# First mixer: low weight parts summed by DMA, and attention outputs weighed by pairs of heads

## The chip, the cores and the metric

The kernel runs on one core of one Trainium2 chip. The metric is the device time of one execution in microseconds (us); a lower time is better. TensorE (PE) does the matrix products, VectorE (DVE), ScalarE (ACT) and GpSimd (POOL) the elementwise work, and SyncE (SP) issues nearly all transfers.

## The reference

A small model of two blocks over 512 tokens of width 1024, all in float32. The first block has two layers; the change is in the first layer's mixer ("even mixer"), cut here to what matters:

```
z = rmsnorm(x) @ w_in                        # 1024 -> 512 (q) + 128 (k) + 128 (v) + 512 (u)
q, k = rope(q), rope(k)                      # 8 query heads, 2 key/value heads, width 64
s = q k^T / 8, only keys with |i - j| <= 128, softmax with one extra sink logit per head
p = exp(s - m) / (sum exp(s - m) + exp(sink - m))
ya = p @ v                                   # 8 heads x 64 = 512 columns
d  = centred mean of u over 2, 4, 8, 16 positions, minus u   # four groups of 128 columns
yb = (d @ w_pool[group]) * pool_scale        # 512 columns
x  = x + concat(ya, yb) @ w_out              # 1024 -> 1024
x  = x + relu(rmsnorm(x) @ w1)^2 @ w2        # 1024 -> 4096 -> 1024
```

A second layer with another mixer, a second block and a final norm follow; the change doesn't touch their code.

## The kernel before

**Products in three parts.** Each float32 factor is split into a high part (rounded to the fp32r type that TensorE takes) and a low part (the rest). A product is the sum of three matmuls, high x high, high x low and low x high (`mm3`, L561 records each), each with 128 weights columns and 512 tokens; in the trace they are `mm<-hi,wh`, `mm<-hi,wl` and `mm<-lo,wh`. Three such matmuls are called a triple here.

**Weight units.** Weights come from memory in units of 128 x 1024 (512 KB; 8 triples). `Unit.load` issues the transfer on SP's queue into one of 4 raw buffers (`wr`). `Unit.split` makes the two parts: a copy with rounding into `wh` (ACT or POOL, whichever the planner reckons sooner done) and then a subtract, raw minus high, into `wl` (DVE or POOL). `Weights.at` hands a unit's columns to the matmuls once `self.ready` covers them.

**Order of work.** Every engine runs its instructions in the order in which this program emits them. A planner (`_Flow`) decides on that order: it has a clock of its own, `fl.now`, which each matmul moves on, and costs for every elementwise instruction. Chains of elementwise work (generators) go on when their due time has come; `yield 0.1` means to look again 0.1 us of the planner's time later.

In the first mixer (phase "a") the main work is attention (`attend` over the eight `job0`), with up to 3 heads in flight. The dense products are the filling, in the list `fill = [q_blocks(), pooling(), out_proj("eout", yhl, 0)]`. `_Flow.run` takes a step of the filling whenever the main work makes no progress; `_Flow.step` tries only `fill[:self.wide]`, and `wide` is 1 in phase "a". Where that first generator can't go on either, the planner lets 0.1 us pass.

**When a unit is split.** The units stand in the list `order` in the order ein2, ein0, ein1, wpool, ein3, ein4, eout0 to eout3. `pump` drops a unit from the head of the list when it has been used up, and starts the split of those among the first three that it can:

```
while order and order[0].task is not None and order[0].left == 0:
    order.pop(0)
...
for i, u in enumerate(order[:AHEAD]):          # AHEAD = 3
```

`Weights.at` starts the split of a unit that is asked for and not yet begun. `wpool` (one unit of 512 columns) holds the matrices of the four pooling groups, one product for each, so it is used up only with the fourth. `pooling` runs over ein3 and ein4, a unit of 8 triples for each group; `pool_chain` then does that group's window sums, the difference, its split into parts, the product with `wpool` (put at the head of `fill`) and the split of the result into `yhl[g]`. The first half of `out_proj` needs all four `yhl[0..3]`, the second half the attention's `yhl[4..7]`.

**A head.** `Head.score` issues the score matmuls (`sc`), `expo` the row maximum (`mx`, `nm`, DVE) and the exponential with its row sum (`p<-sc,nm`, ACT). `finish` then adds the sink's part to the denominator, takes the reciprocal (`w4`) and calls `weigh`, four copies with a scale (`p<-p,w`, ACT or POOL) over blocks of 256 or 384 columns. `apply` waits for that (`self.done`); it transposes the probabilities (`tr<-cst,p`), splits them into parts (`ph` on ACT, `pl` on DVE) and multiplies with the values (`av`). `combine` and `store` gather two heads into one `ya` of 128 x 512 and split it into `yhl[4 + pair]`.

Of the kernel before, what the change touches and what calls it, by code (L numbers as in the profile page):

```python
# [13 lines left out]
AF = mybir.ActivationFunctionType  # L14
ALU = mybir.AluOpType
# [3 lines left out]
P = 128  # L19
# [3 lines left out]
NQ = T // P  # L23
# [33 lines left out]
_WT = {}  # L57
# [431 lines left out]
def tile_hybrid(ctx: ExitStack, tc: tile.TileContext, wt, xT, pT, prm_d, cst_d, out):  # L489
    nc = tc.nc  # L490
# [3 lines left out]
    fl = _Flow()  # L494
    go = fl.go
    V, S, G = (_Engine(fl, e, k) for e, k in ((nc.vector, "V"), (nc.scalar, "S"), (nc.gpsimd, "G")))
# [13 lines left out]
    def uid(s):  # L510
        cnt[0] += 1
        return f"{s}{cnt[0]}"

    def blk(name="b", dt=F32, n=T):
        return bp.tile([P, TB], dt, tag="b", bufs=NB, name=uid(name))[:, 0:n]

    def small(n, name="s", dt=F32):
        return sp.tile([P, n], dt, tag=f"s{n}", bufs=24, name=uid(name))
# [6 lines left out]
    def bank(tag):  # L525
        spare = len(banks) - sum(1 for k in held if k != tag and not held[k])
        if held[tag] >= getattr(fl, tag) or spare < 1 or min(banks) > fl.now:
            return None
        banks.remove(min(banks))
        held[tag] += 1  # L530
        return pp.tile([P, T], F32, tag="ps", bufs=8, name=uid(tag))
# [6 lines left out]
    def takec(tag):  # L538
        while (t := bank(tag)) is None:
            yield 0.1  # L540
        return t

    def give(tag):
        banks.append(max(fl.now, fl.last) + 0.1)
        held[tag] -= 1
# [6 lines left out]
    def waitc(*tasks):  # L552
        for t in tasks:
            while not t.done:
                yield 0.1

    def f(ap):
        return ap.bitcast(F32)
# [5 lines left out]
    def tr(o, i, idn):  # L564
        PE.transpose(o, i, idn)  # L565
        fl.now += 0.11
# [4 lines left out]
    def first(*engines):  # L571

        return min(engines, key=lambda e: max(e[0].free, fl.now) + e[1])[0]

    def width(ap):
        n = 1
        for d in ap.shape[1:]:
            n *= d
        return n

    def copy(out, src, scale=None):

        n, ps = width(out), src.space == PSUM
        sc = 1.0 if scale is None else scale
        e = first((S, 0.06 + n / 1090.0), *(() if ps else ((G, 0.07 + n * 0.00117 + fl.gc),)))
        if e is S:
            S.activation(out, src, AF.Copy, scale=sc)
        else:
            G.tensor_scalar(out, src, sc, 1.0, op0=ALU.mult, op1=ALU.mult)

    def tt(op, out, a, b, bias=None):

        n = width(out)
        if PSUM in (a.space, b.space):
            e = V
        else:
            e = first((V, 0.07 + n / 960.0), (G, 0.07 + n * 0.00227 + (fl.gt if bias is None else bias)))
        e.tensor_tensor(out, a, b, op=op)


    NRAW, NSPLIT, AHEAD = 4, 4, 3
    units, order = {}, []

    class Unit:
        def __init__(self, name, i, cuts=1):
            self.name, self.i = name, i
            t = _WT[name]
            self.n = min(1024, _WN[t][1] - 1024 * i)
            self.left = self.n
            self.raw = self.hi = self.lo = self.task = None  # L610
            self.parts = [(self.n * c // cuts, self.n * (c + 1) // cuts) for c in range(cuts)]
            self.at, self.ready = [], 0
            self.kept = None
# [48 lines left out]
        def split(self):  # L662
            while len(self.at) < len(self.parts):
                self.load()
            r = self.raw
            self.hi = wp.tile([P, 1024], F32R, tag="whi", bufs=NSPLIT, name=uid("wh"))
            self.lo = wp.tile([P, 1024], F32R, tag="wlo", bufs=NSPLIT, name=uid("wl"))
            wl["split"] += 1
            wl["due"] -= 1
            for (c0, c1), t in zip(self.parts, self.at):  # L670
                while fl.now < t:
                    yield 0.1
                copy(self.hi[:, c0:c1], r[:, c0:c1])
                yield
                tt(ALU.subtract, self.lo[:, c0:c1], r[:, c0:c1], f(self.hi[:, c0:c1]), fl.gw)
                if c1 == self.n:
                    wl["raw"] -= 1
                yield
                self.ready = c1

        def use(self, n):
# [4 lines left out]
    wl = {"raw": 0, "split": 0, "dma": 0.8, "due": 0}  # L686
# [89 lines left out]
    def C(name, n=None):  # L776
        o = _CO[name][0]
        n = n or _CO[name][1]
        if o + n <= NKEEP:
            return cst[:, o:o + n]  # L780
        t = blk("cst")
        nc.sync.dma_start(t[:, :n], cst_d[:, o:o + n])
        return t

    def PR(name, i=0, n=1):
        o, w = _PO[name]
        return prm[:, o + i:o + i + n]

    ident = C("ident")
# [42 lines left out]
    def split_to(act, ps, scale=None):  # L832
        act.hi, act.lo = blk("hi", F32R), blk("lo", F32R)
        yield from split_ps(ps, act.hi, act.lo, scale)
        yield
        act.done = True
# [155 lines left out]
    class Head:  # L992
# [2 lines left out]

        def __init__(self, passes, rng, masks, v, scale=1.0, nsink=None, sink=None, gate=None):
            self.passes, self.rng, self.masks, self.v = passes, rng, masks, v
            self.scale, self.nsink, self.sink, self.gate = scale, nsink, sink, gate  # L1000
            self.done = False
            self.join = None

        def expo(self, qbs, ps):
# [44 lines left out]
        def finish(self, tasks):  # L1049

            yield from waitc(*tasks)
            if self.sink is not None:
                es = small(4, "es")
                S.activation(es, self.nm, AF.Exp, bias=self.sink, scale=1.0)
                yield
                V.tensor_add(self.den, self.den, es)
            else:
                V.tensor_scalar(self.den, self.den, 1e-30, None, op0=ALU.max)
            w4 = small(4, "w4")
            V.reciprocal(w4, self.den)  # L1060
            if self.gate is not None:
                V.tensor_mul(w4, w4, self.gate)
            yield
            yield from self.weigh(w4)

        def weigh(self, w4):
            for qb in range(NQ):
# [64 lines left out]
    def combine(po, dst):  # L1132

        t = blk("cmb")
        copy(t[0:64], po[64:128])
        yield
        V.tensor_add(dst, po[0:64], t[0:64])
        give("av")
        yield
# [21 lines left out]
    SC64 = 0.125  # L1161
# [53 lines left out]
    def next_norm(gcol, *sums):  # L1215

        h = acts()

        def then(c):
            go(split_to(h[c], x[c], gcol(c)))  # L1220
            for ss, sc in sums:
                go(ss.add(x[c], None if sc is None else sc(c)))
            yield

        return h, then
# [3 lines left out]
    h = acts()  # L1229
# [26 lines left out]
    nsink = cons.tile([P, 8], F32, name="nsink")  # L1256
# [113 lines left out]
    fill = [q_blocks(), pooling(), out_proj("eout", yhl, 0)]  # L1370
    yz = {}

    def store(hd, base, post=None):

        def done(po):
            i = hd // 2
            if i not in yz:
                yz[i] = [blk("ya"), 0]
            y = yz[i][0]
            yield from combine(po, y[64 * (hd % 2):64 * (hd % 2) + 64])  # L1380
            yz[i][1] += 1
            if yz[i][1] == 2:
                del yz[i]
                if post is not None:
                    yield from post(i, y)
                yield from split_to(yhl[base + i], y)
        return done

    def job0(hd):
        st = {}  # L1390

        def score():
            g = hd // 4
            q = qs[hd]
            st["h"] = Head([(q, ks[g][0]), (q, ks[g][1])], band3, band3_masks, lambda kb: v0[0](kb, g),
                           SC64, nsink=nsink[:, hd:hd + 1], sink=PR("sink", hd))
            return st["h"].score()

        return (lambda: hd in qs and 1 in ks and v0 and nmask.done, score,
                lambda: st["h"].apply(done=store(hd, 4)))  # L1400

    fl.phase("a")
    fl.run(kv_blocks(), None)
# [2 lines left out]
    h, then = next_norm(lambda c: PR("n_mlp0", c), (ss, None))  # L1406
# [99 lines left out]
    h = h2  # L1506
# [256 lines left out]
    def job1(hd):  # L1763
        st = {}

        def score():
            (qh, ql), (kh, kl) = qt[hd], kt[hd]
            st["h"] = Head([(qh, kh), (ql, kh), (qh, kl)], full, {},
                           lambda kb: vt[hd // 2](kb, hd % 2))
            return st["h"].score()  # L1770

        return (lambda: hd in qt and hd in kt and hd // 2 in vt, score,
                lambda: st["h"].apply(done=store(hd, 4)))
# [10 lines left out]
    h, then = next_norm(lambda c: PR("n_mlp1", c), (ss, None))  # L1784
# [15 lines left out]
    h = h2  # L1800
# [588 lines left out]
    h = h2  # L2389
# [26 lines left out]
```

## Time and profile before

| | |
|---|---|
| time, median of 3 runs | 1477.36 us (1476.55 to 1479.11) |
| profiled execution: time, span | 1479.96 us, 1478.2 us |
| mean granted TensorE clock | 0.994 of full |
| busy share of the span: PE, DVE, ACT, POOL | 98%, 61%, 44%, 21% |
| read from HBM, written | 205.26 MB, 84.93 MB |

The profile is of one execution; its time is 2.6 us above the median of the runs. Times in the rows are microseconds from the span's start, durations in us unless ns stands by them. Matmuls are pipelined, so a row's duration is longer than the distance to the next start. "Idle before" in brackets names what ended the idle time of the engine.

### The profile page before, as it was taken

To read this page: it belongs to the slowest core of one execution; us is meant where nothing else is said; L and a number is where in the kernel's file an instruction comes from. 1 tells how busy PE (TensorE), PEld (TensorE's weight loads), DVE (VectorE), ACT (ScalarE), POOL (GpSimd) and SP (SyncE) were. 2 spreads that over 40 slices of the span, in tenths; PEclk is the share of its full clock that TensorE was granted. 3 is DMA by queue.
4 is the path that set the end of the run, shared out by engine and by line. 5 is a ranking of instruction groups with operands and counts; after the bars stand their busy time and mean duration, and the time that the engine had idled before them with its cause. 6 is when DMAs were issued, how large, how long until landed. Compare 5 with 4: busy or idle time off the path is not lost.

```text
span 1478.2 us, 18891 instructions
## 1 busy us (share of the span) xinstructions
PE 1449.5 (98%) x6789; PEld 1174.4 (79%) x6789; DVE 899.0 (61%) x1410; ACT 649.5 (44%) x1192; POOL 310.7 (21%) x291
## 2 busy tenths in 40 slices
PE   8999999999999999899999999999999999999998
PEld 5777878888888888688888888888787788888787
DVE  7896864655434555977775665657755566536413
ACT  5684432433222347487433434334521576324623
POOL 5451220211102013631120210202110000100332
PEclk9999999999999999999999999999999999999999
DMA  6113588888423454333499999999865223346252
GB/s 212 52 44 99 176 291 272 286 290 280 133 95 100 137 213 158 127 129 128 149 318 330 327 330 330 314 336 323 287 216 195 109 86 115 115 182 214 103 196 89
DMA packets 118317, 291.44 MB, mean 197 GB/s; under 512 B 13136, under 2 KB 14672, under 8 KB 118224
## 3 DMA queue, kind: packets, MB, share of 16 engines
q1 hardware_dynamic: 118080, 289.98, 57.9%
q8 instruction: 53, 0.87, 0.2%
q14 instruction: 40, 0.33, 0.1%
q10 hardware_dynamic: 144, 0.26, 0.1%
HBM read 205.26 MB, written 84.93 MB: 196 GB/s over the span
## 4 chain that ended last, share of the span: by engine, by line
PE 83%; DMA 7%; DVE 5%; issue 1%; ACT 1%; SPq 1%; POOL 0%; DVEq 0%; POOLq 0%; ACTq 0%
PE mm L561 72%; PE sc L561 4%; PE av L561 3%; PE tr L565 3%; DMA kr<-in_wt_dram 3%; DMA wk<-klo 2%; PE tr L561 1%; DMA wk<-khi 1%; DVE wl L363 1%; DMA x<-in_xT_dram 1%; ACT wh L363 1%; DVE klo L363 0%; DVE gz L363 0%; DVE sg L363 0%; DMA pin<-in_pT_dram 0%
## 5 line engine op out<-in xcount | busy, mean ns | idle before, releaser
L561 PE MATMUL mm<-hi,wh 128*128 128x512 f32 (+1 forms) x1276 | 509.4, 399 | 0.8 <-POOL wh L363 0.5
L561 PE MATMUL mm<-hi,wl 128*128 128x512 f32 (+1 forms) x1276 | 501.1, 393 | 4.4 <-DVE wl L363 2.6
L561 PE MATMUL mm<-lo,wh 128*128 128x512 f32 (+1 forms) x1276 | 499.3, 391 | 0.3 <-POOL lo L363 0.3
L561 PEld LDWEIGHTS mm<-lo,wh 128*128 128x128 f32 x1276 | 240.4, 188 | 55.6 <-POOL lo L363 0.8
L561 PEld LDWEIGHTS mm<-hi,wl 128*128 128x128 f32 x1276 | 240.8, 189 | 54.9 <-DVE wl L363 3.6
L561 PEld LDWEIGHTS mm<-hi,wh 128*128 128x128 f32 x1276 | 240.9, 189 | 52.9 <-ACT wh L363 1.5
L363 ACT ACTIVATE khi<-kr 128x512 fp32r<-128x512 f32 x120 | 75.8, 632 | 308.8 <-DMA kr<-in_wt_dram 303.1
L561 PE MATMUL mm<-ul,wh 128*128 128x512 f32 x512 | 201.6, 394 | 1.8 <-DVE ul L363 1.8
L561 PE MATMUL mm<-uh,wh 128*128 128x512 f32 x512 | 201.7, 394 | 0.3 <-ACT uh L363 0.3
L561 PE MATMUL mm<-uh,wl 128*128 128x512 f32 x512 | 201.6, 394 | 0.0
L363 DVE TENSOR_TENSOR wl<-wr,wh 128x1024 fp32r<-128x1024 f32 (+1 forms) x145 | 184.5, 1273 | 6.4 <-ACT wh L363 4.8
L363 DVE TENSOR_TENSOR klo<-kr,khi 128x512 fp32r<-128x512 f32 x150 | 124.3, 830 | 87.7 <-ACT khi L363 77.3
L363 ACT ACTIVATE wh<-wr 128x1024 fp32r<-128x1024 f32 (+1 forms) x147 | 148.8, 1013 | 47.8 <-PE mm L561 34.4
L363 DVE TENSOR_TENSOR x<-x,mm 128x512 f32<-128x512 f32 x112 | 76.8, 686 | 151.0 <-PE mm L561 146.3
L363 POOL TENSOR_TENSOR ma<-ma 128x512 f32<-128x512 f32 x62 | 85.4, 1377 | 282.7 <-ACT uh L363 232.2
L561 PEld LDWEIGHTS mm<-ul,wh 128*128 128x128 f32 x512 | 96.2, 188 | 25.2 <-DVE ul L363 2.9
L561 PEld LDWEIGHTS mm<-uh,wh 128*128 128x128 f32 x512 | 96.1, 188 | 23.1 <-ACT uh L363 0.7
L561 PEld LDWEIGHTS mm<-uh,wl 128*128 128x128 f32 x512 | 96.2, 188 | 22.3
L363 ACT ACTIVATE p<-sc,nm 128x512 f32<-128x512 f32 (+3 forms) x136 | 75.2, 557 | 30.4 <-DVE nm L363 27.3
L363 DVE TENSOR_TENSOR pl<-tr,ph 128x512 fp32r<-128x512 f32 (+2 forms) x108 | 66.5, 623 | 25.4 <-ACT ph L363 24.8
L363 POOL TENSOR_SCALAR khi<-kr 128x512 fp32r<-128x512 f32 x30 | 28.6, 953 | 250.3 <-DMA kr<-in_wt_dram 214.1
L363 DVE SCALAR_TENSOR_TENSOR ma<-mm,rb 128x512 f32<-128x512 f32 x64 | 44.1, 688 | 52.4 <-PE mm L561 52.2
(290 smaller groups left out, 1619.0 us busy)
## 6 DMA issues: line engine op xcount, KB each, us to landing
wr<-in_wt_dram SPq DMA_DIRECT2D x144, 512.0 KB, 5.3
kr<-in_wt_dram SPq DMA_DIRECT2D x150, 256.0 KB, 5.9
wk<-khi SPq DMA_DIRECT2D x150, 256.0 KB, 5.9
wk<-klo SPq DMA_DIRECT2D x150, 256.0 KB, 5.7
wh<-wk SPq DMA_DIRECT2D x74, 512.0 KB, 3.3
wl<-wk SPq DMA_DIRECT2D x74, 512.0 KB, 4.2
x<-xs SPq DMA_DIRECT2D x16, 256.0 KB, 5.1
cst<-in_cst_dram SPq DMA_DIRECT2D x8, 256.0 KB, 5.4
```

The lines of the kernel that those rows point to most:

```text
L363: return fn(*a, **k)
L561: PE.matmul(o, l, r, start=start, stop=stop, skip_group_check=True)
L565: PE.transpose(o, i, idn)
```

## The change

Two edits in the first mixer. For the 12 units of ein3, ein4 and eout0 to eout3, `split` no longer subtracts: ACT copies the raw unit with a scale of -1 and rounding into `wl`, the copy into `wh` stays, and a transfer issued on GpSimd's queue then reads the unit from memory a second time and adds it onto `wl`, which leaves raw minus high there. The planner takes the unit as ready at least 7.0 us after that issue. And the probabilities of the first mixer's heads are no longer weighed: a head counts as done when its exponentials are, its `w4` goes into a tile for two heads (`w8`), and `weigh_pair` spreads that tile over 128 x 512 by one ACT copy, transposes it by four TensorE transposes and multiplies the pair's `ya` with it on DVE, ahead of `ya`'s split.

```
--- before.py
+++ after.py
@@ -599,6 +599,7 @@
 
 
     NRAW, NSPLIT, AHEAD = 4, 4, 3
+    ADDED = ("ein3", "ein4", "eout0", "eout1", "eout2", "eout3")
     units, order = {}, []
 
     class Unit:
@@ -670,12 +671,25 @@
             for (c0, c1), t in zip(self.parts, self.at):
                 while fl.now < t:
                     yield 0.1
-                copy(self.hi[:, c0:c1], r[:, c0:c1])
-                yield
-                tt(ALU.subtract, self.lo[:, c0:c1], r[:, c0:c1], f(self.hi[:, c0:c1]), fl.gw)
-                if c1 == self.n:
-                    wl["raw"] -= 1
-                yield
+                if self.name in ADDED:
+
+                    S.activation(self.lo[:, c0:c1], r[:, c0:c1], AF.Copy, scale=-1.0)
+                    copy(self.hi[:, c0:c1], r[:, c0:c1])
+                    if c1 == self.n:
+                        wl["raw"] -= 1
+                    yield
+                    c = 1024 * self.i
+                    nc.gpsimd.dma_start(self.lo[:, c0:c1], wt[_WT[self.name], :, c + c0:c + c1], accum_op=ALU.add)
+                    G.free = max(G.free, fl.now) + 1.0
+                    wl["dma"] = max(wl["dma"], fl.now) + 3.0
+                    yield max(7.0, wl["dma"] + 4.0 - fl.now)
+                else:
+                    copy(self.hi[:, c0:c1], r[:, c0:c1])
+                    yield
+                    tt(ALU.subtract, self.lo[:, c0:c1], r[:, c0:c1], f(self.hi[:, c0:c1]), fl.gw)
+                    if c1 == self.n:
+                        wl["raw"] -= 1
+                    yield
                 self.ready = c1
 
         def use(self, n):
@@ -995,10 +1009,12 @@
 
 
 
-        def __init__(self, passes, rng, masks, v, scale=1.0, nsink=None, sink=None, gate=None):
+
+        def __init__(self, passes, rng, masks, v, scale=1.0, nsink=None, sink=None, gate=None, w4=None):
             self.passes, self.rng, self.masks, self.v = passes, rng, masks, v
             self.scale, self.nsink, self.sink, self.gate = scale, nsink, sink, gate
-            self.done = False
+            self.w4 = w4
+            self.done = self.weighed = False
             self.join = None
 
         def expo(self, qbs, ps):
@@ -1049,6 +1065,7 @@
         def finish(self, tasks):
 
             yield from waitc(*tasks)
+            self.done = self.w4 is not None
             if self.sink is not None:
                 es = small(4, "es")
                 S.activation(es, self.nm, AF.Exp, bias=self.sink, scale=1.0)
@@ -1056,12 +1073,14 @@
                 V.tensor_add(self.den, self.den, es)
             else:
                 V.tensor_scalar(self.den, self.den, 1e-30, None, op0=ALU.max)
-            w4 = small(4, "w4")
+            w4 = small(4, "w4") if self.w4 is None else self.w4
             V.reciprocal(w4, self.den)
             if self.gate is not None:
                 V.tensor_mul(w4, w4, self.gate)
             yield
-            yield from self.weigh(w4)
+            self.weighed = True
+            if self.w4 is None:
+                yield from self.weigh(w4)
 
         def weigh(self, w4):
             for qb in range(NQ):
@@ -1370,6 +1389,24 @@
     fill = [q_blocks(), pooling(), out_proj("eout", yhl, 0)]
     yz = {}
 
+    def weigh_pair(heads, w8):
+
+        def post(i, y):
+            while not all(h.weighed for h in heads):
+                yield 0.1
+            t = blk("wb")
+            S.activation(t.rearrange("p (b h e) -> p b h e", b=NQ, h=2),
+                         w8.rearrange("p (h b) -> p b h", h=2).unsqueeze(3).to_broadcast([P, NQ, 2, 64]), AF.Copy)
+            yield
+            ps = yield from takec("tr")
+            for b in range(NQ):
+                tr(ps[:, b * P:(b + 1) * P], t[:, b * P:(b + 1) * P], ident)
+            yield
+            V.tensor_mul(y, y, ps)
+            give("tr")
+            yield
+        return post
+
     def store(hd, base, post=None):
 
         def done(po):
@@ -1386,18 +1423,23 @@
                 yield from split_to(yhl[base + i], y)
         return done
 
+    pairs = [([], small(8, "w8")) for _ in range(4)]
+
     def job0(hd):
         st = {}
+        heads, w8 = pairs[hd // 2]
 
         def score():
             g = hd // 4
             q = qs[hd]
             st["h"] = Head([(q, ks[g][0]), (q, ks[g][1])], band3, band3_masks, lambda kb: v0[0](kb, g),
-                           SC64, nsink=nsink[:, hd:hd + 1], sink=PR("sink", hd))
+                           SC64, nsink=nsink[:, hd:hd + 1], sink=PR("sink", hd),
+                           w4=w8[:, 4 * (hd % 2):4 * (hd % 2) + 4])
+            heads.append(st["h"])
             return st["h"].score()
 
         return (lambda: hd in qs and 1 in ks and v0 and nmask.done, score,
-                lambda: st["h"].apply(done=store(hd, 4)))
+                lambda: st["h"].apply(done=store(hd, 4, weigh_pair(heads, w8))))
 
     fl.phase("a")
     fl.run(kv_blocks(), None)
```

## Rows read from the trace of the kernel before

**Rows 1.** The page's busy times: us, share of the span, instructions.
```profile
PE 1449.5 (98%) x6789; PEld 1174.4 (79%) x6789; DVE 899.0 (61%) x1410; ACT 649.5 (44%) x1192; POOL 310.7 (21%) x291
```
**Rows 2.** Windows, dense matmuls alone: stretch, length, PE busy (count), clock, DMA share, GB/s.
```profile
54.37:71.97 17.60, 13.26 (x51) 1.00 0.11 31
71.97:74.64 2.67, 0.16 (x2) 1.00 0.01 3
74.64:85.33 10.69, 7.05 (x27) 1.00 0.16 51
85.33:88.49 3.16, 0.64 (x2) 1.00 0.00 0
88.49:97.03 8.54, 7.04 (x26) 1.00 0.18 61
97.03:101.42 4.39, 0.64 (x3) 1.00 0.01 2
101.42:103.38 1.96, 1.96 (x8) 1.00 0.48 107
103.38:114.18 10.80, 1.29 (x5) 1.00 0.14 44
114.18:125.11 10.93, 9.32 (x34) 1.00 0.37 131
125.11:159.94 34.83, 34.83 (x151) 1.00 0.29 88
```
**Rows 3.** The chain that ended last, a piece: start, length, instructions.
```profile
125.11 34.83 PE mm L561 x150
```
**Rows 4.** PE's timeline from 84 to 128: start, duration, form, count, idle before.
```profile
88.49 0.50 PE L561 MATMUL mm<-hi,wl 128*128 128x512 f32 x1 [0.59 <-DVE wl L363]
...
101.42 0.50 PE L561 MATMUL mm<-hi,wl 128*128 128x512 f32 x1 [0.60 <-DVE wl L363]
...
106.98 0.39 PE L561 MATMUL av<-pl,v 128*128 128x256 f32 x1 [0.40 <-DVE pl L363]
...
108.88 0.50 PE L561 MATMUL mm<-lo,wh 128*128 128x512 f32 x1 [0.32 <-POOL lo L363]
...
111.53 0.44 PE L561 MATMUL av<-ph,v 128*128 128x384 f32 x1 [0.42 <-ACT ph L363]
113.90 0.45 PE L561 MATMUL av<-pl,v 128*128 128x384 f32 x1 [1.93 <-DVE pl L363]
...
119.90 0.93 PE L565 MATMUL tr<-cst,p 128*128 128x128 f32 x7
```
**Rows 5.** Timeline of all engines from 71.9 to 74.7.
```profile
72.34 1.05 ACT L363 ACTIVATE wh<-wr 128x1024 fp32r<-128x1024 f32 x1
...
73.43 1.23 DVE L363 TENSOR_TENSOR wl<-wr,wh 128x1024 fp32r<-128x1024 f32 x1
```
**Rows 6.** Timeline of all engines from 107.9 to 111.5.
```profile
108.80 1.05 POOL L363 TENSOR_SCALAR wh<-wr 128x1024 fp32r<-128x1024 f32 x1
...
111.13 2.24 DVE L363 TENSOR_TENSOR wl<-wr,wh 128x1024 fp32r<-128x1024 f32 x1 [0.57 <-ACT wh L363]
```
**Rows 7.** Groups by form, 20 to 160 (two queries): count, busy us, mean ns.
```profile
L363 ACT ACTIVATE wh<-wr 128x1024 fp32r<-128x1024 f32 x16 | 16.8, 1049 | 4.8 <-issue 3.9 <-DMA wr<-in_wt_dram 0.9
...
L363 ACT ACTIVATE p<-p,w 128x384 f32<-128x384 f32 x13 | 7.8, 607 | 0.0
...
L363 ACT ACTIVATE p<-p,w 128x256 f32<-128x256 f32 x10 | 5.0, 505 | 2.2 <-DVE w L363 2.2
...
L363 DVE TENSOR_TENSOR wl<-wr,wh 128x1024 fp32r<-128x1024 f32 x17 | 25.3, 1490 | 0.8 <-ACT wh L363 0.6
```
**Rows 8.** DMA issues from 0 to 165: queue, count, KB each, median us to landing.
```profile
wr<-in_wt_dram SPq DMA_DIRECT2D x23, 512.0 KB, 4.0
```
**Rows 9.** Windows of PE around 610: length, busy (count), granted clock, DMA share, GB/s.
```profile
610.00:614.00 4.00, 0.00 (x0) 0.63 0.00 0
614.00:618.00 4.00, 3.14 (x10) 0.52 0.00 0
```

## Prediction

> **What bounds the kernel now.** I read the page first: PE is busy for 98% of the span [rows 1]. A gain can only come from time in which PE stands still, and any stall that the change makes counts in full. The change lies in the first mixer, so the next view is the one by windows, cut where the dense matmuls stop and start [rows 2]. The reader is to see a pattern there: the filling runs (51, 27, 26 matmuls), and between these runs lie stretches with 2, 2, 3 and 5 dense matmuls, in which PE has only attention: 71.97 to 74.64, 85.33 to 88.49, 97.03 to 101.42, 103.38 to 114.18. From 125.11 on the chain of waits shows 150 matmuls in 34.83 us without a break [rows 3]: 0.232 us each, the price used below.
>
> The timeline of PE gives the stalls in that part [rows 4]. Six idle gaps add up to 0.59 + 0.60 + 0.40 + 0.32 + 0.42 + 1.93 = 4.26 us. At each gap PE loses some 0.2 us more, because a row of 0.39 to 0.50 us normally overlaps the next start, 0.232 us on. So 4.26 + 6 x 0.22 = 5.6 us are lost. Three gaps wait for `wl` or for `pl`, which stood behind a `wl` of 2.24 us on DVE; one waits for a `lo` on POOL.
>
> **Why the filling stops.** The timeline of all engines at 72 tells [rows 5]. The unit of ein4's first block is copied at 72.34 and subtracted at 73.43, only after the filling stopped at 71.97. `pump` could not start it: `wpool` stands at the head of `order` until the fourth pooling product, so the first three places stay `wpool`, ein3, ein3, and each later unit is begun only when `Weights.at` asks for it. Once the fourth pooling product is on its way, two units start at once, on POOL at 108.80 and on ACT before the 2.24 us `wl` [rows 6]. With `wide` = 1 no other filling is tried meanwhile. So three of the 12 units (ein4's two, eout0's first) are made while the filling waits.
>
> **The change part by part.**
>
> *Removed.* Twelve subtracts, 11 on DVE at a mean of 1.49 us [rows 7] (the 17 of that row less four of ein0 and ein1 and two of the MLP's first weights), one on POOL. Also 32 weighing copies, 23 on ACT (7.8 + 5.0 = 12.8 us) [rows 7], the rest on POOL. None of it runs on PE; what it can give is the 5.6 us of stalls. I credit all of it: three of the six gaps, with 3.12 of the 4.26 us, are the subtracts' own [rows 4, 6], and the others lie on the same busy engines.
>
> *Added to PE.* 4 pairs x 4 transposes. Seven of that form take 0.93 us [rows 4]; with the last one's tail taken off, 0.109 us each: 16 x 0.109 = 1.75 us. Everything around is dense, so they cost that in full. The ACT copy (4) and the DVE product (4) per pair follow a head's last `av`; the second half of out_proj, which needs them, starts some 54 matmuls (12.5 us) after attention's end. If that cover is gone they cost about 2 us once.
>
> *Added to ACT.* 12 negated copies of 1.05 us [rows 7], forced onto ACT: 12.6 us, against the 12.8 us that leave it. ACT ends about even, and the `wh` copy can move to POOL (1.05 us there too [rows 6]). I put this at nothing; its cover is that ACT isn't the last wait in five of the six gaps.
>
> *Moved onto GpSimd's queue.* 12 transfers of 512 KB. Each waits in POOL's order for ACT's negated copy; behind it stand POOL's window sums (`us`) and `lo`, which the pooling chain needs. SP's queue loses nothing and gets raw buffers back earlier. The extra 6.3 MB meet transfer engines that are 0 to 48% busy [rows 2], so bandwidth is free.
>
> *The wait that is added.* A unit was ready 1.23 us after `wh` [rows 5]; now the planner holds it for at least 7.0 us after the issue. For a unit asked for on the spot the filling stops for 0.4 (72.34 less 71.97) + 1.05 + 0.1 + 7.0 = 8.55, say 8.6 us, where it was 2.67 and 3.16 us [rows 2]. No transfer of this kind stands in the trace. The nearest row is the plain load of the same bytes, 4.0 us to landing [rows 8]. That is the lower bound; the upper I set at 10 us, two plain loads and 2 us for the queue ahead. I take the planner's 7.0, for PE's order is written by it.
>
> By the Trainium skill ("DMA: Bandwidth & Descriptors", section on the anatomy of a DMA on the GpSimd path) such a transfer takes 2.0 us plus bytes / 436,000, which for 512 KB makes an estimate of 3.2 us; it has no price for the addition. By that the wait would be shorter than the plan's, and the third rival would gain.
>
> *What fills the wait.* From 54.37 to 125.11 (70.74 us) stand 158 dense matmuls [rows 2], 36.7 us, and 5.6 us of stalls. The rest, 28.4 us, is attention; with the transposes 30.2. While the filling runs attention takes its share: 17.60 - 51 x 0.232 = 5.8, 10.69 - 27 x 0.232 = 4.4, 8.54 - 26 x 0.232 = 2.5, together 12.7 us [rows 2]. So 17.5 us are left for three waits: ein4's first block, ein4's second, and eout0's first, which falls together with the fourth group's pooling chain. 3 x 8.6 = 25.8 us. Attention runs out in the third: 25.8 - 17.5 = 8.3 us with nothing for PE to do. In the kernel before the same stretches were served because they were short, and attention lasted to 125.
>
> *The clock.* After an idle stretch (610 to 614, no matmul) the granted clock was 0.63 and then 0.52, about the lower level of 1.2 GHz [rows 9]. Six matmuls at half speed lose some 1.2 us; I add half of it, 0.6 us, since the idle time may come in pieces.
>
> *The dense stretch after attention* keeps its cover: with `wpool` gone, `pump` starts a unit two units ahead, 2 x 24 x 0.232 = 11.1 us, more than 8.6.
>
> *The sum:* + 8.3 + 0.6 + 1.75 - 5.6 = + 5.05 us. Against the profiled execution's own 1479.96 that is 1485.0; that one lies 2.6 us above the median of the runs, and against the median it is **1482.4 us**.
>
> **The rivals.**
>
> 1. *Attention lasts through the waits; the old stalls go.* Without `weigh` a head's chain is shorter and DVE has 16 us less to do, so attention may be spread such that the waits are filled. For it: from 54.37 to 159.94, 105.6 us, PE's work is 105.6 - 5.6 = 100.0 us, 101.7 with the transposes, so there is room. Against it: a shorter chain makes attention run out earlier, not later. Idle time near 0: 1.75 - 5.6 = - 3.85, **1473.5 us**. It decides if attention's share beside the filling falls from 12.7 to some 5 us.
> 2. *The sum is in early.* With 4.0 us instead of 7.0 the first two waits shrink by 3 us each on the chip; the third stays, since the pooling chain holds it. 8.3 - 6 = 2.3 us idle; 2.3 + 1.75 - 5.6 = - 1.55: **1475.8 us**, no difference to be told. For it: rows 8. Against it: PE's order stays as planned, and attention has been used up by then all the same.
> 3. *The sum is late.* At 10 us three waits grow by 3 us each: + 9 on the forecast, **1491 us**. The dense stretch would then just hold (1.05 + 10 against 11.1). For it: the addition must read what it adds to, and POOL can be late with the issue.
>
> **How the numbers follow.** Chances: forecast 0.50, rival 1 0.25, rival 2 0.16, rival 3 0.09. About 0.2% (3 us) is what a measurement of this kernel tells from no change. Faster by more: 0.23 of rival 1 and 0.02 of rival 2, 0.25. Within: 0.13 of rival 2, 0.04 of the forecast, 0.02 of rival 1, 0.19. Slower: 0.46 of the forecast, 0.09 of rival 3, 0.01 of rival 2, 0.56. The forecast's own range is 1478.5 to 1487 (idle 4.4 to 12.7 us, the latter where attention's share rises by 4.4). The range for 8 in 10 reaches down to rival 1's time and up to half of rival 3's surplus: 1473.5 to 1488.5 us.
>
> **What would show it.** Right: three stretches of 7 to 9 us without dense matmuls between 70 and 125, the last with PE idle for over 5 us waiting for the added transfer or for the pooling chain, and a granted clock below 1.0 there; the gaps behind `wl` on DVE gone; the issues on GpSimd's queue landing 5 to 8 us after. Attention would end earlier than at 125, the out projection later than at 160. Wrong: PE without gaps from 54 to 160 (rival 1), landings near 4 us with idle time under 3 us (rival 2), `mm<-hi,wl` waiting in the dense stretch too (rival 3), or later stages moving by more than 3 us, which this sum doesn't hold.

## The result, and the profile after

The changed kernel takes 1497.32 us (median of 4 runs, 1493.35 to 1500.48), the kernel before in the same series 1478.23 us (4 runs, 1476.55 to 1481.48). The ratio is 1.0126, with a 95% interval of 1.0100 to 1.0152: slower by 19 us, where 1482.4 us was forecast, and outside the range. The profiled execution took 1496.84 us (span 1495.0), 16.9 us more than that of before, and that difference is what its trace must explain.

Where it arises can be seen by taking the 5,388 dense matmuls of both traces in order and comparing their starts. At the 100th (40 us) the changed kernel is 2.1 us ahead; at the 400th (149.3 us in the trace of before) it is 15.5 us behind; at the last one 16.8 us. So the loss of the first mixer from 40 us on is 17.6 us, and the rest of the program adds 1.3 us.

The page's busy times, to be set beside [rows 1]:

```profile
PE 1457.5 (97%) x6805; PEld 1180.4 (79%) x6805; DVE 896.0 (60%) x1409; ACT 641.2 (43%) x1174; POOL 319.2 (21%) x298
```

PE has 16 instructions more, the transposes. DVE and ACT are less busy and the time is longer, so their total busy time didn't set it. The windows of the dense matmuls, cut where they stop and start, answer to [rows 2] (columns as there):

```profile
54.12:75.69 21.57, 14.30 (x51) 1.00 0.24 49
75.69:86.08 10.39, 0.17 (x1) 1.00 0.46 103
86.08:98.21 12.13, 7.41 (x27) 1.00 0.00 1
98.21:111.92 13.71, 0.17 (x1) 0.94 0.34 79
111.92:121.16 9.24, 8.73 (x27) 0.72 0.24 28
121.16:126.91 5.75, 0.00 (x1) 0.74 0.60 137
126.91:131.06 4.15, 4.15 (x10) 0.54 0.50 83
131.06:175.37 44.31, 43.20 (x187) 1.00 0.74 177
```

The filling runs 51, 27 and 27 matmuls, much as before (51, 27, 26), but the stops between these runs are now 10.39, 13.71 and 5.75 us long. The same stretches for all that PE does show how full attention kept it in the first two:

```profile
75.69:86.08 10.39, 8.87 (x61) 1.00 0.46 103
...
98.21:111.92 13.71, 8.28 (x50) 0.94 0.34 79
```

PE stands idle for 1.5 us of the first stop, 5.4 us of the second and all 5.75 us of the third. Behind the second and the third stop the granted clock is 0.72 and 0.54 on average, with dense matmuls some 0.43 us apart instead of 0.23 (112.35, 112.77 and 113.20 below): the lower of the two levels, 1.2 GHz.

The timeline of all engines shows what each stop waits for:

```profile
77.44 1.05 ACT L363 ACTIVATE wl<-wr 128x1024 fp32r<-128x1024 f32 x1
...
78.79 0.89 POOL L682 DMA_DIRECT2D wl<-in_wt_dram  x1 [11.37 <-DVE up L363]
...
102.08 1.05 ACT L363 ACTIVATE wl<-wr 128x1024 fp32r<-128x1024 f32 x1
...
103.00 0.39 PE L561 MATMUL av<-pl,v 128*128 128x256 f32 x1 [1.60 <-DVE pl L363]
...
103.43 0.88 POOL L682 DMA_DIRECT2D wl<-in_wt_dram  x1 [0.56 <-ACT wl L363]
...
108.21 1.58 POOL L363 TENSOR_TENSOR lo<-ya,hi 128x512 fp32r<-128x512 f32 x1 [1.84 <-ACT hi L363]
...
108.59 1.24 DVE L363 TENSOR_TENSOR ed<-us,cst 128x16 f32<-128x16 f32 x1
...
109.85 1.04 POOL L363 TENSOR_SCALAR wh<-wr 128x1024 fp32r<-128x1024 f32 x1
109.86 1.05 DVE L363 TENSOR_TENSOR pd<-ed,up 128x16 f32<-128x16 f32 x1
110.83 0.55 DVE L363 TENSOR_TENSOR pl<-tr,ph 128x384 fp32r<-128x384 f32 x1
...
111.43 0.69 PE L561 MATMUL av<-pl,v 128*128 128x384 f32 x1 [2.51 <-DVE pl L363]
...
112.35 0.63 PE L561 MATMUL mm<-hi,wl 128*128 128x512 f32 x1
...
112.77 0.63 PE L561 MATMUL mm<-lo,wh 128*128 128x512 f32 x1
...
113.20 0.63 PE L561 MATMUL mm<-hi,wh 128*128 128x512 f32 x1
...
121.20 0.69 DVE L363 TENSOR_TENSOR up<-mm,rb 128x512 f32<-128x512 f32 x1 [3.55 <-PE mm L561]
...
126.91 0.80 PE L561 MATMUL mm<-hi,wh 128*128 128x512 f32 x1 [5.75 <-ACT hi L363]
```

The first two stops are ein4's two units, begun only when asked for: the negated copy comes 1.75 and 3.87 us after the filling stopped (75.69 and 98.21), the issue 1.35 us after the copy's start, the landing 7.7 and 7.6 us after the issue. In the second stop PE goes on only 0.9 us after that landing (111.04), because an `av` of attention stands ahead in its queue and waits for `pl` until 111.43. The third is the fourth group's pooling chain, from `up` at 121.20 to its product at 126.91. The last `av` starts at 111.43; before it was at 124.78. So nothing of attention was left to run under that chain.

The DMA issues from 0 to 175 (columns as in [rows 8]):

```profile
wr<-in_wt_dram SPq DMA_DIRECT2D x22, 512.0 KB, 5.0
wl<-in_wt_dram POOLq DMA_DIRECT2D x12, 512.0 KB, 7.8
```

And in the chain that ended last, where [rows 3] had 34.83 us without a break, an added transfer stands ahead of the dense stretch:

```profile
128.10 8.37 DMA wl<-in_wt_dram
136.52 43.60 PE mm L561 x187
```

**A sum that all kernels below share.** For each form of PE instruction (operation, tile, columns) I take the usual distance to the next start (the 30th percentile of the whole run) and add up, from 54 to 160 us, what single distances exceed it by: above 0.245 us as stalls, from 0.04 to 0.245 us as slow issue, which is where a lower clock shows (but not only: before has 2.1 us of it at a clock of 1.00). Before: 6.9 us of stalls, 2.1 us slow. After: 17.8 and 6.6. So + 10.8 stalls + 4.5 slow + 1.75 for the transposes = + 17.1 us, of the 17.6 that the first mixer lost. Of the 17.8 us of stalls 15.0 lie in the three stops. Of the 6.6 us of slow issue 3.6 lie where the granted clock was 0.50 (110.3 to 117.1 and 123.9 to 130.7); the other 3.0 lie at a clock of 1.00.

### The profile page after: what moved, and what is told of

It reads as the page before. It is cut to its first block, busy times and chain, and to the rows that moved or that the text cites. A ratio compares the mean times of both kernels' runs of the same rounds, so it can differ in the third digit from the quotient of the medians.

```text
span 1495.0 us, 18919 instructions
## 1 busy us (share of the span) xinstructions
PE 1457.5 (97%) x6805; PEld 1180.4 (79%) x6805; DVE 896.0 (60%) x1409; ACT 641.2 (43%) x1174; POOL 319.2 (21%) x298
## 3 DMA queue, kind: packets, MB, share of 16 engines
q0 software_dynamic: 1728, 6.29, 2.2%
## 4 chain that ended last, share of the span: by engine, by line
PE 81%; DMA 8%; DVE 5%; issue 3%; ACT 1%; POOL 1%; SPq 1%; POOLq 0%; DVEq 0%; ACTq 0%
PE mm L561 70%; DMA kr<-in_wt_dram 4%; PE sc L561 4%; PE tr L565 3%; PE av L561 3%; DMA wl<-in_wt_dram 1%; DMA wk<-khi 1%; PE tr L561 1%; DVE wl L363 1%; DVE sg L363 0%; DVE q L363 0%; ACT wh L363 0%; DMA pin<-in_pT_dram 0%; DVE kl L363 0%; POOL khi L363 0%
## 5 line engine op out<-in xcount | busy, mean ns | idle before, releaser
L363 DVE TENSOR_TENSOR wl<-wr,wh 128x1024 fp32r<-128x1024 f32 (+1 forms) x134 | 168.0, 1254 | 4.9 <-ACT wh L363 3.5
L363 ACT ACTIVATE wh<-wr 128x1024 fp32r<-128x1024 f32 (+1 forms) x136 | 137.3, 1010 | 43.4 <-PE mm L561 34.2
L363 ACT ACTIVATE p<-sc,nm 128x512 f32<-128x512 f32 (+3 forms) x136 | 75.1, 556 | 35.4 <-DVE nm L363 30.2
L363 POOL TENSOR_SCALAR khi<-kr 128x512 fp32r<-128x512 f32 x30 | 32.1, 1069 | 249.5 <-DMA kr<-in_wt_dram 207.3
```

The source lines that it names most:

```text
L363: return fn(*a, **k)
```

## The experiments

| kernel | us, median | ratio to before, 95% interval | stalls, slow (us) |
|---|---|---|---|
| whole change | 1497.32 | 1.0126 (1.0100 to 1.0152) | 17.8, 6.6 |
| weighing by pairs alone | 1492.86 | 1.0091 (1.0075 to 1.0108) | 17.4, 5.6 |
| transfers alone | 1493.73 | 1.0099 (1.0080 to 1.0118) | 16.0, 9.6 |
| weighing, transfers for ein3 and eout1 to 3 | 1486.13 | 1.0046 (1.0029 to 1.0063) | 11.7, 5.8 |
| whole, units begun ahead | 1478.62 | 0.9994 (0.9982 to 1.0005) | 6.7, 3.9 |
| before, units begun ahead | 1475.89 | 0.9982 (0.9973 to 0.9992) | 5.2, 2.8 |
| weighing, units begun ahead | 1483.78 | 1.0038 (1.0025 to 1.0052) | 10.7, 5.6 |
| transfers, units begun ahead | 1479.41 | 1.0006 (0.9996 to 1.0016) | 5.7, 3.0 |
| weighing, heads held | 1479.95 | 1.0014 (1.0004 to 1.0024) | 8.5, 3.3 |
| whole, heads held | 1491.45 | 1.0093 (1.0075 to 1.0110) | 15.0, 7.1 |
| whole, both remedies | 1476.37 | 0.9992 (0.9980 to 1.0004) | 4.5, 3.0 |
| weighing, both remedies | 1476.42 | 0.9994 (0.9985 to 1.0004) | 4.3, 3.3 |
| whole, zeros in the planned waits | 1502.44 | 1.0170 (1.0151 to 1.0189) | 7.0, 6.4 |

The medians of before were 1478.2, 1479.2, 1478.7 and 1477.9 us in the four series. In the last column the zeros' own time doesn't count as a stall.

**One edit at a time.** The weighing by pairs alone:

```
-    ADDED = ("ein3", "ein4", "eout0", "eout1", "eout2", "eout3")
+    ADDED = ()
```

> Only the weighing by pairs; all units are subtracted as before. Theory A (three units that are asked for on the spot wait some 10 us each for the added transfer, and attention alone can't fill that): within 4 us of the kernel before, 1474 to 1480 us. Rival B (the shorter chain of a head packs attention so tightly that DVE can't follow, and it runs out early): most of the 19 us is here, 1490 us or more.

And the added transfers alone, heads weighed as before:

```
                            SC64, nsink=nsink[:, hd:hd + 1], sink=PR("sink", hd),
-                           w4=w8[:, 4 * (hd % 2):4 * (hd % 2) + 4])
-            heads.append(st["h"])
+                           SC64, nsink=nsink[:, hd:hd + 1], sink=PR("sink", hd))
...
-                lambda: st["h"].apply(done=store(hd, 4, weigh_pair(heads, w8))))
+                lambda: st["h"].apply(done=store(hd, 4)))
```

> Only the 12 added transfers; the probabilities are weighed as before. Theory A: most of the loss is here, 1488 to 1495 us, with three stretches of 9 to 14 us without dense matmuls between 70 and 130. Rival B: at most 1483 us.

Measured: + 13.7 us for the one and + 14.6 us for the other, + 19.1 us for both. Each of the two theories explained one kernel and missed the other. So the change has two harmful edits. Their losses overlap (28.3 us if they added up), as they would if both used up the same cover; that this is why is not shown. The trace of the weighing alone has no added transfer and still ends its first mixer like the whole change does. Its timeline, all engines:

```profile
83.86 0.80 PE L561 MATMUL mm<-hi,wl 128*128 128x512 f32 x1 [1.88 <-DVE wl L363]
...
124.18 2.65 POOL L363 TENSOR_TENSOR wl<-wr,wh 128x1024 fp32r<-128x1024 f32 x1
124.56 2.31 DVE L363 TENSOR_TENSOR ed<-us,cst 128x16 f32<-128x16 f32 x1
...
127.79 0.79 PE L561 MATMUL mm<-hi,wh 128*128 128x512 f32 x1 [5.96 <-ACT hi L363]
```

Attention's last `av` starts at 119.56, and PE waits 5.96 us for the fourth pooling chain, as in the whole change. At 83.86 it waits for a subtract on the spot, which attention used to cover.

**Transfers only where a unit is begun ahead.** ein4's and eout0's units are subtracted as before:

```
+    ADDED = ("ein3", "eout1", "eout2", "eout3")
```

> Both edits, but ein4 and eout0 (the units that are asked for on the spot, and one more) are subtracted as before; 8 units keep the added transfer. Theory A: the loss goes nearly all, 1474 to 1481 us. Rival B: 1490 us or more, since the weighing stays. Rival C (the transfer lands late in the dense stretch): 1485 us or more, with waits of mm<-hi,wl after 120.

Measured + 7.0 us, between A and B, and about half of what the weighing alone loses. The time lies in C's range, but C's sign is missing: no `mm<-hi,wl` waits after 120 in its trace. The longest waits of PE there, 1.99 and 1.83 us (122.27 and 125.48), are for `hi` from ACT.

**Units begun ahead of time.** In `pump`, used-up units leave `order` wherever they stand, so that `wpool` at its head no longer keeps ein4's units and eout0's first out of the first three places:

```
-        while order and order[0].task is not None and order[0].left == 0:
-            order.pop(0)
+        order[:] = [u for u in order if u.task is None or u.left > 0]
```

> The changed kernel, but a used-up unit leaves the list wherever it stands in it, so that wpool no longer keeps ein4 and eout0 from being begun ahead. All 12 transfers and the weighing stay. Theory A: 1474 to 1482 us, the waits before ein4's two units under 3 us each. Rival B: 1490 us or more.

With the whole change the time is that of before (- 0.5 us): all of the 19.1 us come back. PE's longest marked wait from 54 to 140 us is now 1.42 us. Its busy time from 54.37 to 159.94 (windows, all of PE), for the changed kernel and then here:

```profile
54.37:159.94 105.57, 91.54 (x457) 0.94 0.44 100
...
54.37:159.94 105.57, 101.44 (x523) 1.00 0.52 117
```

The same edit of `pump` in the kernel before and with each edit of the change alone:

> The kernel before, with nothing of the change, but with used-up units taken out of the order wherever they stand, so that ein4's units and eout0's first are begun ahead of time. Theory A (units begun only when asked for are what stops the filling): three stops of about 3 us that attention covered go away and with them part of the 4.4 us of idle PE between 40 and 160; 1474 to 1478 us. Theory B (what counts is how long attention lasts beside the filling): no stop was exposed before, so 1477 to 1481 us, not to be told from before.

> The added transfers alone (probabilities weighed as before), with units begun ahead. Theory A: the 14 us of the transfers alone were stops of the filling, and are gone, 1475 to 1481 us. Theory C (the added transfer itself is too slow for the dense stretch, or the engines' share costs): 1485 us or more.

> The weighing by pairs alone (no added transfer), with units begun ahead. Theory A: the 14 us of the weighing alone came through units made on the spot, and with these gone the time is that of before or a little below, 1474 to 1481 us. Theory B: a shorter head chain lets attention run out early whatever the units do, so most of the 14 us stays, 1487 us or more.

Before gains 2.8 us by it, as theory A had it. The transfers then are not told from the kernel before (+ 0.7 us), as theory A had it for them. Against the kernel before with the same edit, which was measured beside them, they still cost 3.5 us, and these two intervals lie apart. So most of their 14.6 us is gone where a unit is begun early, but not all. The weighing keeps 5.1 of its 13.7 us (7.9 against before with the same edit), so A doesn't hold for it; B's bound of 1487 us was missed as well.

**Heads held.** What else could the weighing have taken away? It took four copies out of the time before a head counts as done. Here a head is held for four planned steps of 0.6 us without any work in them:

```
             self.weighed = True
             if self.w4 is None:
                 yield from self.weigh(w4)
+            else:
+                for _ in range(NQ):
+                    yield 0.6
+                self.done = True
```

(and `self.done` is no longer set ahead of that). With the weighing alone, units begun as before:

> The weighing by pairs alone, units begun as before, but each head is called done four planned steps of 0.6 us after its sums, about the time that the four weighing copies took, without any work in them. Theory A: units made on the spot still stop the filling, 1487 us or more. Theory B: attention is spread beside the filling as it was before, so the 14 us go, 1476 to 1482 us.

Measured + 1.2 us: waiting 2.4 planned us for nothing gives back 12.5 us. Theory B holds for the weighing. Dense matmuls from 54.37 to 97.03 (windows) say how it works. The kernel before and the weighing alone:

```profile
54.37:97.03 42.66, 28.16 (x105) 1.00 0.12 38
...
54.37:97.03 42.66, 23.23 (x78) 0.96 0.08 25
```

And with the heads held:

```profile
54.37:97.03 42.66, 27.73 (x102) 1.00 0.11 38
```

A head that is ready earlier gives attention more to do, and the filling gets fewer of the planner's steps: attention's first `av` starts at 59.26 us instead of 67.51, and 252 dense matmuls instead of 294 have started when attention ends. With the heads held it is 67.72 us and 291. The fourth pooling chain, which only the filling brings on, then stands alone.

**Both together.** The whole change with the heads held:

> The whole change, with each head called done four planned steps of 0.6 us later, and units begun as before. Theory A (two causes, one for each edit): the hold takes back only what the shorter head chain cost, and the transfers' stops of the filling stay, so about the time of the transfers alone, 1490 to 1496 us. Theory B (one cause, attention running out early): attention spread as before fills the transfers' stops too, 1480 to 1487 us.

It is about as slow as the transfers alone: 1491.45 us, + 13.6 where these had + 14.6. So in the whole change the hold gives back 5.5 us. It cures the weighing and nothing else, as theory A had it; the stops for units begun on the spot stay. In the timeline of PE one of them shows as a wait for the added transfer itself:

```profile
101.69 0.50 PE L561 MATMUL mm<-hi,wl 128*128 128x512 f32 x1 [2.06 <-DMA wl<-in_wt_dram]
```

With both remedies, the whole change and the weighing alone:

> The whole change with both remedies, units begun ahead and heads held. Theory A: the remedies take away one cause each and add up; below the 1478.6 us of units begun ahead alone, 1474 to 1478 us. Theory B: with the units begun ahead nothing is left that the hold could cure, 1477.5 to 1481 us.

> The weighing by pairs alone, with both remedies. Theory A: 1483.8 us with units begun ahead and 1480.0 us with heads held become 1475 to 1479 us, the gain of units begun ahead on the kernel before (2.8 us) coming on top of the hold. Theory B: one of the two cures all that can be cured, 1479 to 1482 us.

1476.37 and 1476.42 us, both in theory A's range. For the weighing alone the remedies add up: + 5.1 with the one, + 1.2 with the other, - 1.5 us with both. For the whole change that can't be told: - 0.5 us with units begun ahead and - 1.5 us with both, each against the median of before in its own series, and the intervals overlap. From 54 to 140 us PE's timeline of the whole change with both remedies has six marked waits, together 2.8 us. The longest is 0.84 us at 108.28, for `hi` from ACT; the next two are these:

```profile
54.85 1.13 PE L561 MATMUL tr<-zs,cst 128*128 128x512 f32 x2 [0.65 <-ACT zs L363]
...
97.54 0.55 PE L565 MATMUL tr<-cst,p 128*128 128x128 f32 x3 [0.78 <-DVE ya L363]
```

Neither is told from before, and neither beats the kernel before with units begun ahead (0.9982). That one line is the only version here whose interval lies below 1.

**The clock.** Where the plan of the changed kernel has nothing to issue in the first mixer, a matmul of zeros that nothing reads is issued, 107 in all. Each writes one of the buffers of the dense products, if the planner (`spin`) finds one free:

```
     def idle(self, us=0.1):
+        if self.spin is not None and self.spin():
+            us = 0.22
         self.now += us
```

> The whole change as it is, but where the plan finds nothing to issue in the first mixer, a matmul of zeros (bf16, 128x512) that nothing reads goes to TensorE; 107 of them, 64 of them after the last dense matmul before the third and fourth stop. Clock theory: the granted clock stays at 1.00 from 100 to 131 and the 4.8 us that matmuls 0.43 us apart lose there come back, 1491 to 1494.5 us. Rival: the clock's fall only shows where PE would wait anyway, and the zeros take PE's time themselves, 1496 us or more.

Windows of all PE's work in the changed kernel, then here, and then of the zeros alone:

```profile
100.00:120.00 20.00, 14.57 (x64) 0.83 0.30 62
120.00:140.00 20.00, 13.14 (x49) 0.83 0.78 178
...
100.00:120.00 20.00, 19.94 (x120) 1.00 0.24 54
120.00:140.00 20.00, 18.43 (x84) 1.00 0.56 118
...
100.00:120.00 20.00, 5.76 (x18) 1.00 0.24 54
120.00:140.00 20.00, 9.97 (x43) 1.00 0.56 118
```

The granted clock stays at 1.00 from 100 to 140, where it was 0.83: with PE kept busy there, the fall is gone. It falls elsewhere, to 0.84 on average from 84 to 94, behind another idle stretch:

```profile
89.16 1.27 PE L841 MATMUL mm<-spun 128*128 128x512 bf16 x4 [2.47 <-DVE ya L363]
```

There the zeros themselves wait, and the scores of attention (90.08) stand behind them in PE's queue. The time is 5 us longer than that of the whole change, in the rival's range. That zeros ahead of work are the reason is argued from such rows and not shown. So the test shows what the clock's fall follows, and not what the fall costs in all. By the shared sum the slow issue at the lower clock was 3.6 us, and not the 4.8 us expected.

## Why the prediction was right in direction and wrong in size

**Right.** Three stretches without dense matmuls stand between 70 and 127; the third is the pooling chain with PE idle for 5.75 us (over 5 had been named); the granted clock falls behind them; the transfers land in 7.8 us at the median (5 to 8 had been named, and single ones took up to 13.5); attention ends at 111 instead of 125; later stages move by 1.3 us (less than 3). The transposes stand at 1.75 us: 4 in 0.66 us at the full clock, with the last one's tail. The plain load of [rows 8] was rightly taken for a lower bound only.

By the Trainium skill ("DMA: Bandwidth & Descriptors", anatomy of a DMA on the GpSimd path) the estimate was 3.2 us; the trace disagrees, with 7.8 us for the accumulating form. The prediction says there that the third rival would gain by so short a wait; it is the second that would have.

**Wrong: the step "What fills the wait".** It took attention as a stock of 17.5 us that fills the first two waits completely and leaves 8.3 us of idle time in the third. Three things in it failed.

*Attention alone doesn't fill PE.* In [rows 2] it ran nearly without gaps because it stood beside dense matmuls and for 2 to 4 us at a time; the long stretch there, 103.38 to 114.18, has four of the six stalls of [rows 4], which was the warning. In stops of 10 and 14 us attention waits for its own chain through ACT and DVE: 1.5 and 5.4 us idle, 2.51 of these for a `pl` that stood behind `ed` and `pd` (last section). In the prediction's sum this moves idle time from the third stop to the others; how much it is in all comes from the next two points.

*The waits are longer than 8.6 us.* 0.4 us was taken from the filling's stop to the first copy. It was 1.75 and 3.87 us, because the copy is put behind what ACT already has from attention. The first two stops took 10.39 + 13.71 us where the sum had 17.2; the third, 5.75, was shorter than its 8.6. Together they are 29.85 us instead of 25.8.

*Attention's share beside the filling isn't 12.7 us.* That came from [rows 2] and was carried over unchanged, though the change itself moves it. "A shorter chain makes attention run out earlier" stood only as an objection to the first rival and had no term in the sum. With 0.232 us for each matmul, attention's share beside the first two runs was 21.57 - 51 x 0.232 = 9.7 and 12.13 - 27 x 0.232 = 5.9 us, together 15.6; at the third run attention was over. So of its 30.2 us only 14.6 were left for the stops, and not 17.5.

Put into the prediction's own sum, 29.85 - 14.6 makes 15.2 us without work in place of 8.3, and the stalls measured in the three stops are 15.0. Of the 6.9 us that are too much, 4.0 come from the length of the stops and 2.9 from attention's share. On its own the share weighs more: by the kernels with heads held and not held it is worth 12.5 us of the weighing's 13.7, where the sum counts the weighing as + 1.75 us less some part of 5.6. In the whole change, where the losses overlap, holding the heads gives back 5.5 us.

**Wrong: the credit of - 5.6 us.** All the stalls of before were struck out. In the changed kernel 2.7 us of stalls stand outside the three stops, where before had 6.9 in all: - 4.2. With both remedies, where nothing else that the trace shows is lost, stalls go from 6.9 to 4.5 us and the time by - 1.5 us, which isn't told from nothing, while before with units begun ahead falls by 2.8 us without any part of the change. Other waits take the place of the old ones (`hi`, `ya` and `lo` instead of `wl`).

**Wrong: the clock's + 0.6 us.** The sum had half of six matmuls, and no row gives the six. At the granted clock of 0.50 17 dense matmuls and three other instructions came late, 3.6 us in all, after two idle stretches. The other 0.9 us by which slow issue grew don't lie at the lower clock.

In the terms of the prediction: stalls + 10.8 instead of + 2.7 (15.0 less 4.2 in place of 8.3 less 5.6), clock + 3.6 instead of + 0.6, other slow issue + 0.9 instead of nothing, transposes + 1.75 as said. Of the rivals, the first (1473.5, no stalls left) describes the kernel with both remedies best, which took 1476.4; the third (a late landing) didn't come about as described: 7.8 us is near the planned 7.0, and 1.1 us is lost to a landing in the dense stretch, at 136 (2.6 us with the transfers alone and with the heads held). Two of the three stops did grow as it said, but mainly because the copies came late. The upper end of the range, 1488.5 us, doesn't follow from its rule: half of rival 3's surplus on the forecast gives 1486.9.

**What stays open.** With units begun ahead, the whole change (0.9994 of before) is faster than the weighing alone (1.0038), while the transfers make the kernel before slower, by 3.5 us; whether the subtracts that go from DVE are the reason, no run separates. Where those 3.5 us are lost isn't known either: the stalls and slow issue of the two kernels differ by 0.6 us. No run was made for the blocking described below. It isn't the main cause: with the whole change and heads held no operation is stretched by it, and 13.6 us are lost.

## What to carry to other kernels

Work that covers a wait is a stock and a rate: ask how long it lasts, how full it keeps the engine when it runs alone, and whether the change itself makes it run out sooner. Making the covering work's chain shorter can cost time where the order gives the rest only the gaps; here 2.4 planned us of doing nothing were worth 12.5 us. A slower way of making an operand is cheap if it is begun early (3.5 us here) and dear if it is begun on demand (14.6 us), so look first at when the work is begun: one line in the order of the units undid the loss.

## What the hardware showed that I had not expected

**Small DVE operations held for the length of a POOL instruction.** `ed` and `pd` on 128x16 take 0.17 us in most places, and in the fence of the changed kernel's timeline 1.24 and 1.05 us, ending with POOL's `lo` (108.21 + 1.58) and `wh` (109.85 + 1.04); behind them stands the `pl` for which PE waits 2.51 us. With the weighing alone `ed` takes 2.31 us beside POOL's `wl` of 2.65 us. With `den` on 128x4 the first mixer has 16 such operations in each trace. In the trace of before none begins while a POOL instruction runs, and none is stretched; in the others none to four are. Of the 24 in all traces that take over 0.3 us, 23 begin while a POOL instruction runs and end within 0.04 us of its end.

The Trainium skill ("SBUF — State Buffer", "Who interferes with whom") says that a DVE instruction with two inputs in SBUF contends with a GpSimd instruction that reads SBUF, and that the second to come waits for the whole of the first; these rows agree.

**The added transfer's price.** 512 KB that are added to what stands there took 7.6 to 8.4 us (medians) to land in the kernels with all 12 of them (7.3 to 13.5 us in the changed kernel, the longest where three were issued between 128.1 and 130.7), where the plain load takes 4.0 us in the kernel before and about 5 us beside the added ones. From 40 to 175 us of the changed kernel the queues show what it takes of the transfer engines (packets, MB, share):

```profile
q0 software_dynamic: 1728, 6.29, 24.5%
q1 hardware_dynamic: 2068, 7.55, 21.3%
```

Per byte that is 1.4 times the plain load: 24.5 / 6.29 against 21.3 / 7.55.
